# A hybrid decoder layer: reordering the opening's queues, and tying the users of side transfers to TensorE's place

## The chip, the cores and the metric

The kernel runs on one NeuronCore of a Trainium2 chip. The metric is the device time of one execution, in microseconds (us). The core has five engines with an instruction queue each, which work in order: PE (TensorE, the matmuls; its weight loads are listed as PEld), DVE (VectorE), ACT (ScalarE), POOL (GpSimd) and SP (SyncE). Transfers between HBM and the on-chip buffers (DMA) are issued from the queues of SP, ACT and POOL. An engine's waiting issue holds up everything behind it in that queue.

## The reference

One layer of a decoder over 2048 positions and 1024 channels, in 32-bit floats. Cut to what matters:

```python
mod = silu(c) @ w_ada + b_ada
shift, scale, gate = split(mod, 3)
h = rms_norm(x, norm_g) * (1 + scale) + shift
hq, hf, hi, hz, rq, rk, rv, rz, ga, gb = split(h @ w_in, offsets)     # ten column groups, 9216 columns
uA = head_rms_norm(hgrn2(silu(hq), lb + (1 - lb) * sigmoid(hf), hi)) * silu(hz)
uB = head_rms_norm(retention(rotary(rq), rotary(rk), rv)) * silu(rz)
m = sigmoid(ga) * uA + sigmoid(gb) * uB
out = rms_norm(x + gate * (m @ w_out), final_g)
```

`hgrn2` is a gated linear recurrence with 8 heads of 128 channels, `retention` a recurrence with a fixed decay for each of 8 heads. Both are computed in chunks.

## The kernel before

**Numbers and products.** Each 32-bit operand of a large product is split into two parts in a rounded format, hi and lo: ScalarE rounds (L340, `b<-w` or `A<-h`), VectorE subtracts (L341). A product is three matmuls, hi x hi, hi x lo and lo x hi.

**Quads.** The combined projection is cut into quads: for each half of the sequence (1024 positions, two blocks of 512) and for each head or pair of heads, a block of columns named by kind (a, v, b, A, B) and number. The string `ORDER` gives their order within a half. Quad 0 (`a0`) is computed as plain products in `opening()`. Every later quad takes seven products of combined operands in place of eight (`seq` lists them). The combinations of h are called A11, A12, A22, S1 to S4; those of the weights are summed in place by `Weights.add` (L466). Each product is four steps of three matmuls, and its result is evicted by `after` (L528 on ScalarE; L541, L548, L552 on VectorE) and handed to `deliver`.

**What sets the order.** TensorE's instructions keep the order in which the program traces them (class `InOrder`; `PE.last` is the latest). The queues of the other engines are ordered when the program is built: a planner simulates the execution and lets each engine take, of the instructions that are ready in that simulation, the one with the lowest place. Three means steer it:

- `tc.high_priority(offset=n)` moves what is traced inside n places ahead.
- `pin(ins)` (`tc.keep_in_program_order`) puts an instruction behind whatever was traced before it on its own engine.
- `behind(ins, pe)` puts an instruction behind a given one, here one of TensorE's. `tc.issue_after(ins)` does so for everything traced inside the block on the engine of `ins`. Both give an order of issue in the planner's simulation and no wait on the chip.

**The opening.** For each of the eight 128-row tiles of the first half, `stats` squares and sums a row tile on ScalarE (L1185); POOL makes 1/rms and a diagonal matrix of it (L186, L189, L1188). `turned` multiplies rows by that diagonal on TensorE (`xps`), which transposes and normalizes at once, and ScalarE applies scale and shift (L1210). These come from `ada`: VectorE multiplies a tile of `w_ada` (`wa`, 512 KB, loaded on SP by `ada_load`) by silu(c) broadcast to all partitions (`scb`, from `row_of_c`: eight products `dgs` at L387, a matmul `scp`, two copies at L393), with a running sum (L400, L404). `prepare(tb, s)` does this for block tb and the s-th channel tile of the order `KO`. Then `plain_step` multiplies with quad 0's weights `wp`, which `plain_split` loads on ScalarE's queue and splits. In the same loop quad 1's first two products run. At the end `deliver` evicts quad 0 (sigmoids at L625, scalings at L627 and L630, products at L635) and frees the banks.

**Buffers.** `tp` has six tiles of 512 columns that side work and evictions share, `mu` four, `r` six for raw weights (`NR`), `bw` three for split weights.

**Side work.** `Background.tick` is called at each product step; after every four it advances each generator in `side` by one `yield`. `next_h(1)` makes the second half's h in the first half: it loads x (`xt`), squares it on ScalarE (L1109), loads the transposed x (`xT`), multiplies (L1125) and scales it, stores it, loads it again and combines it (L1145 to L1161). `ada_row(0)` and `ada_row(1)`, in the second half, make the row `gate`: for each of eight tiles they load 256 KB (`wg`, L1322), yield twice, and add weight times silu(c) to an accumulator (L1328).

The rotary tables of each b quad (`ct`, `sn`) are loaded on POOL's queue into `tp` tiles.

Of the kernel before, what the change touches and what calls it, by code (L numbers as in the profile page):

```python
# [10 lines left out]
F32R = mybir.dt.float32r  # L11
# [52 lines left out]
def tile_hybrid(ctx: ExitStack, tc: tile.TileContext, a: dict, out: bass.AP):  # L64
# [268 lines left out]
    def halves(t):  # L333
        return t[:, 0, :], t[:, 1, :]

    def a_tile(name):
        return halves(apool.tile([P, 2, 512], F32R, name=name, tag="A", bufs=NA))

    def split_into(t, src):
        S.activation(out=t[0], in_=src, func=AF.Copy)  # L340
        return V.tensor_tensor(out=t[1], in0=src, in1=t[0], op=ALU.subtract)  # L341

# [28 lines left out]
    mods = cpool.tile([P, 2 * KT], F32, name="mods", tag="mods")  # L371

    def ada_load(kt):
        made = []
        for i in range(2):
            w = apool.tile([P, 1024], F32, name=f"wa{kt}_{i}", tag="A", bufs=NA)
            nc.sync.dma_start(out=w, in_=a["w_ada"][kt, i])
            made.append(w)
        return made

    def row_of_c():
        scb = apool.tile([P, 1024], F32, name="scb", tag="A", bufs=NA)
        dgs = apool.tile([P, 1024], F32, name="dgs", tag="A", bufs=NA)
        for i in range(2):
            dg = dgs[:, i * 512 : (i + 1) * 512]
            for k4 in range(4):
                V.tensor_scalar(  # L387
                    out=dg[:, k4 * P : (k4 + 1) * P], in0=ident, scalar1=sc[:, 4 * i + k4 : 4 * i + k4 + 1], scalar2=None,
                    op0=ALU.mult,
                )  # L390
            ps = bank(f"scp{i}", ("v", "lv")[i])
            PE.matmul(out=ps, lhsT=ones, rhs=dg, start=True, stop=True)
            V.tensor_copy(out=scb[:, i * 512 : (i + 1) * 512], in_=ps)  # L393
        return scb
# [33 lines left out]
    class Weights:  # L428
# [36 lines left out]
        def add(self, out, x, y):  # L465
            V.tensor_tensor(out=out, in0=x, in1=y, op=ALU.add)  # L466

# [628 lines left out]
    def next_h(sb):  # L1096
        for tb in range(NBLK):
            b = sb * NBLK + tb
            rb = tmp(f"rb{b}")
            for t in range(4):  # L1100
# [7 lines left out]
                for i in range(2):  # L1108
                    pin(S.activation(out=xt[i], in_=xt[i], func=AF.Square, accum_out=ss[:, i : i + 1]))  # L1109
                r = upool.tile([P, 2], F32, name=f"xr{b}_{t}", tag="rr", bufs=4)  # L1110
# [9 lines left out]
            for kt in range(KT):  # L1120
                x = tmp(f"xT{b}_{kt}")
                nc.sync.dma_start(out=x, in_=a["x_t"][kt, :, b * BLK : (b + 1) * BLK])
                for _ in range(3):
                    yield
                pin(V.tensor_tensor(out=x, in0=x, in1=rb, op=ALU.mult))  # L1125
                S.activation(out=x, in_=x, func=AF.Identity, scale=amul[kt], bias=modp[kt])
                htd[tb, kt] = dram(f"hT{b}_{kt}", [P, 512])
                nc.sync.dma_start(out=htd[tb, kt], in_=x)
        for j in range(4):
# [14 lines left out]
            yield  # L1144
            pin(V.tensor_tensor(out=h22, in0=h21, in1=h22, op=ALU.subtract))  # L1145
            keep("S1", h22)
# [3 lines left out]
            yield  # L1150
            pin(V.tensor_tensor(out=h21, in0=h11, in1=h21, op=ALU.subtract))
            keep("S3", h21)
# [6 lines left out]
            yield  # L1159
            pin(V.tensor_tensor(out=h12, in0=h12, in1=h11, op=ALU.add))  # L1160
            keep("S4", h12)  # L1161
# [12 lines left out]
    def opening():  # L1174
# [71 lines left out]

        was = {0: ada_load(0), 4: ada_load(4)}
        for t in range(4):
            stats(t)
        for t in range(4, 8):  # L1250
            load_rows(t)
        plain = {}
# [11 lines left out]

        for b in (0, 1):
            plain_split(b)
        prepare(0, 0)
        for b in (2, 3):
            plain_split(b)
        W.load()  # L1270
        W.split(part_tile("b1_1", "cc", NCC))
        W.split(halves(upool.tile([P, 2, 512], F32R, name="b2_1", tag="af", bufs=1)))
        two = pp.tile([P, 2, 512], F32, name="c01_y1", tag="rt", bufs=1)
        acc = {(0, 0): bank("c00", "o"), (1, 0): bank("c10", "o"), (1, 1): bank("c11", "x0"), (0, 1): two[:, 0, :]}
        xb[1], yb[1] = bank("x1", "x1"), two[:, 1, :]
        for s in range(KT + 2):
            if s < 2:
                for t in (4 + 2 * s, 5 + 2 * s):
                    stats(t)
            if s == 5:  # L1280
                tables()
# [4 lines left out]
            if 0 <= s - 1 < KT:  # L1286
                prepare(1, s - 1)
            if s < KT:
                kt = KO[s]
                for ch in range(2):  # L1290
                    plain_step(acc[ch, 0], 2 * (kt // 4) + ch, ats[0, kt], kt)
                m, j = 1 + kt // 4, kt % 4
                product_step(yb[1] if m == 2 else xb[1], m, 1, j, j == 0, j == 3)
# [10 lines left out]
        for ch, tb in ((0, 0), (1, 1), (1, 0), (0, 1)):  # L1304
            with tc.high_priority(offset=FIRSTS if ch else PEV):
                deliver(0, ch, tb, acc[ch, tb])
# [11 lines left out]
    def ada_row(j):  # L1318
        acc = upool.tile([P, 512], F32, name=f"acc{j}", tag="mu", bufs=4)
        for kt in range(KT):  # L1320
            w = tmp(f"wg{j}_{kt}")
            nc.sync.dma_start(out=w, in_=a["w_gate"][j, kt])  # L1322
            yield
            yield
            if kt == 0:
                V.tensor_scalar(out=acc, in0=w, scalar1=sc[:, 0:1], scalar2=None, op0=ALU.mult)
            else:
                V.scalar_tensor_tensor(out=acc, in0=w, scalar=sc[:, kt : kt + 1], in1=acc, op0=ALU.mult, op1=ALU.add)  # L1328
        bgt = tmp(f"bg{j}")
# [234 lines left out]
```

## Time and profile before

| | |
|---|---|
| runs | 2019.73, 2016.7, 2019.8 us; median 2019.73 |
| profiled execution | 2015.04 us; span from first to last instruction 2013.3 us |
| granted TensorE clock, mean | 0.993 |
| busy TensorE | 1930.3 us |
| busy VectorE, ScalarE, POOL | 1420.3, 985.7, 296.6 us |
| moved by DMA | 259.97 MB |

The profile is of one execution. An engine's idle time is put down to the instruction or transfer that ended it. A number after L is a line of the kernel. Times within the span count from its first instruction. A granted clock under 1.00 in a stretch means that TensorE's matmuls ran slower there.

### The profile page before, as it was taken

The numbers are of one execution on the slowest core, as the hardware profiler recorded it, in microseconds if no ns is written. First come the engines' busy times: TensorE is split into PE (matmuls) and PEld (weight loads), VectorE is DVE, ScalarE is ACT, GpSimd is POOL, SyncE is SP. The second block draws the span as 40 slices with busy tenths as digits, with TensorE's granted clock in tenths as the row PEclk, the third lists the DMA queues.
The fourth block names the chain that finished last, engine by engine and source line by source line (L and its number), as shares of the span: only waits on it lengthen the run. The fifth ranks groups of instructions, "written<-read, shape, count | busy, mean of one in ns | idle before, by whom it ended". The sixth has DMA issues, their size and how long they took to land.

```text
span 2013.3 us, 40043 instructions
## 1 busy us (share of the span) xinstructions
PE 1930.3 (96%) x15172; PEld 1581.7 (79%) x15172; DVE 1420.3 (71%) x2677; ACT 985.7 (49%) x2426; POOL 296.6 (15%) x522
## 2 busy tenths in 40 slices
PE   5799899999999999999999999989999999999998
PEld 4578788887788778888888788878788888887887
DVE  6796767666767777778977676777767775878332
ACT  5635444554556446556444545544454446454321
POOL 2002210211113211201002110211021102010000
PEclk9999999999999999999999999999999999999999
DMA  9335524354354564546544433454435433336442
GB/s 301 78 92 137 134 60 117 102 133 123 112 162 118 133 159 150 168 149 219 134 116 130 112 89 93 121 136 146 111 100 132 114 79 117 91 115 201 152 145 84
DMA packets 453122, 259.97 MB, mean 129 GB/s; under 512 B 171713, under 2 KB 406209, under 8 KB 452929
## 3 DMA queue, kind: packets, MB, share of 16 engines
q1 hardware_dynamic: 286752, 172.89, 30.3%
q10 hardware_dynamic: 153120, 76.04, 13.4%
q0 software_dynamic: 13056, 8.47, 1.7%
q8 instruction: 120, 1.97, 0.4%
q14 instruction: 74, 0.60, 0.1%
HBM read 188.03 MB, written 69.21 MB: 128 GB/s over the span
## 4 chain that ended last, share of the span: by engine, by line
PE 82%; DMA 8%; DVE 5%; ACT 2%; issue 1%; POOL 1%; SPq 1%; ACTq 0%; POOLq 0%; DVEq 0%
PE x L77 33%; PE v L77 17%; PE ops L77 9%; PE y L77 8%; PE E L77 4%; PE lv L77 3%; PE R L77 3%; PE uT L80 2%; DMA rd<-c 1%; DMA ud<-ur 1%; DVE b L341 1%; DVE w L466 1%; PE F L77 1%; DMA sn<-lin 1%; ACT b L340 1%
## 5 line engine op out<-in xcount | busy, mean ns | idle before, releaser
L341 DVE TENSOR_TENSOR b<-w,b 128x512 fp32r<-128x512 f32 (+1 forms) x553 | 346.8, 635 | 228.1 <-ACT b L340 219.5
L340 ACT ACTIVATE b<-w 128x512 fp32r<-128x512 f32 (+1 forms) x553 | 317.1, 583 | 298.3 <-PE x L77 243.0
L77 PE MATMUL x<-S,b 128*128 128x512 f32 x1704 | 432.5, 399 | 7.7 <-DVE c L548 7.7
L77 PE MATMUL v<-S,b 128*128 128x512 f32 x1704 | 424.3, 397 | 3.4 <-ACT c L528 2.4
L77 PE MATMUL x<-A,b 128*128 128x512 f32 x1704 | 421.6, 395 | 0.9 <-DVE c L552 0.9
L77 PEld LDWEIGHTS v<-S,b 128*128 128x128 f32 x1704 | 317.6, 190 | 72.0 <-ACT c L528 3.5
L77 PEld LDWEIGHTS x<-A,b 128*128 128x128 f32 x1704 | 315.7, 188 | 67.5 <-ACT m L345 1.3
L77 PEld LDWEIGHTS x<-S,b 128*128 128x128 f32 x1704 | 312.5, 189 | 70.6 <-DVE c L548 7.0
L77 PE MATMUL y<-A,b 128*128 128x512 f32 x840 | 208.3, 396 | 1.0 <-DVE ro L695 0.8
L466 DVE TENSOR_TENSOR w<-w,w 128x512 f32<-128x512 f32 x284 | 195.4, 688 | 9.6 <-DMA w<-in_w_b_dram 4.8
L186 POOL TENSOR_SCALAR ssh<-ssh 128x1 f32<-128x1 f32 x128 | 51.2, 400 | 999.5 <-ACT uh L883 999.4
L77 PEld LDWEIGHTS y<-A,b 128*128 128x128 f32 x840 | 155.9, 189 | 35.3 <-issue 1.8
L77 PE MATMUL ops<-wo,m 128*128 128x512 f32 x768 | 174.5, 390 | 0.0
L77 PEld LDWEIGHTS ops<-wo,m 128*128 128x128 f32 x768 | 144.1, 188 | 29.8
L528 ACT ACTIVATE c<-v 128x512 f32<-128x512 f32 x142 | 84.6, 596 | 149.6 <-PE v L77 134.4
L888 ACT ACTIVATE uh<-E,rrh 128x128 f32<-128x128 f32 x128 | 47.3, 369 | 111.6 <-POOL rrh L189 97.4
L77 PEld LDWEIGHTS lv<-q,k 128*32 128x32 f32 (+1 forms) x5888 | 70.2, 109 | 37.6 <-issue 28.5
L189 POOL TENSOR_TENSOR rrh<-ssh,mhalf 128x1 f32<-128x1 f32 x128 | 97.7, 763 | 10.6
L548 DVE TENSOR_TENSOR c<-c,x 128x512 f32<-128x512 f32 x71 | 48.8, 687 | 63.8 <-PE x L77 63.6
L77 PE MATMUL lv<-q,k 128*32 128x16 f32 (+2 forms) x5888 | 81.3, 188 | 11.8 <-DVE k L856 5.6
L855 DVE TENSOR_TENSOR q<-q,f 128x512 f32<-128x512 f32 x112 | 77.9, 695 | 8.9 <-PE lv L77 8.5
L528 ACT ACTIVATE c<-y 128x512 f32<-128x512 f32 x70 | 41.8, 597 | 73.7 <-PE y L77 73.6
(191 smaller groups left out, 2431.7 us busy)
## 6 DMA issues: line engine op xcount, KB each, us to landing
w<-in_w_d_dram ACTq DMA_DIRECT2D x128, 256.0 KB
w<-in_w_c_dram ACTq DMA_DIRECT2D x66, 256.0 KB
mu<-ud SPq DMA_DIRECT2D x64, 256.0 KB
w<-in_w_a_dram ACTq DMA_DIRECT2D x60, 256.0 KB
wa<-in_w_ada_dram SPq DMA_DIRECT2D x16, 512.0 KB
w<-in_w_b_dram ACTq DMA_DIRECT2D x32, 256.0 KB
vd<-vt SPq DMA_DIRECT2D x128, 64.0 KB
vh<-vd SPq DMA_DIRECT2D x64, 128.0 KB
```

What stands on the lines that cost most here:

```text
L77: return self.kept(nc.tensor.matmul(**kw))
L80: return self.kept(nc.tensor.transpose(**kw))
L186: G.tensor_scalar(out=ss, in0=ss, scalar1=n * EPS, scalar2=None, op0=ALU.add)
L189: G.tensor_tensor(out=dst, in0=ss, in1=mhalf.broadcast_to([P, w]), op=ALU.pow)
L340: S.activation(out=t[0], in_=src, func=AF.Copy)
L341: return V.tensor_tensor(out=t[1], in0=src, in1=t[0], op=ALU.subtract)
L466: V.tensor_tensor(out=out, in0=x, in1=y, op=ALU.add)
L528: S.activation(out=t, in_=ps, func=AF.Copy)
L548: V.tensor_tensor(out=t, in0=t, in1=xb[q], op=ALU.subtract)
L855: V.tensor_tensor(out=qv, in0=qv, in1=tv[:, :, :, 0:1].broadcast_to([P, NU, nb, m]), op=ALU.mult)
L888: behind(S.activation(out=dsts[i], in_=pos[i], func=AF.Copy, scale=rr[:, i : i + 1]), PE.last)
```

## The change

1. **The opening's queues.** The first channel tile's two `wa` loads are traced at high priority, so that they may go first on SP; the second pair and the last four row tiles of x are queued behind them on SP. All four plain weights are loaded and split before the first `prepare`, with their VectorE subtractions queued behind the last of the `dgs` products; quad 1's raw weights are loaded there too. Quad 1's first two splits are queued behind the first A tile's two parts, on VectorE and on ScalarE.
2. **The sums of quad 1's weights** (`Weights.add`, while fewer than eight splits are done) are placed behind TensorE's latest instruction at step 2 of the opening's loop.
3. **The end of the opening.** What `deliver` puts on ScalarE's queue for quad 0 is queued behind the rounding of the last tile of h that `prepare` made.
4. **Users of side transfers.** In `next_h` and `ada_row` the instruction that first uses a loaded tile is placed behind TensorE's latest instruction.
5. **The gates' weights.** `ada_row` yields four times between load and use, not twice.

No arithmetic changes.

```diff
     def split_into(t, src):
-        S.activation(out=t[0], in_=src, func=AF.Copy)
-        return V.tensor_tensor(out=t[1], in0=src, in1=t[0], op=ALU.subtract)
+        parted["hi"] = S.activation(out=t[0], in_=src, func=AF.Copy)
+        parted["lo"] = V.tensor_tensor(out=t[1], in0=src, in1=t[0], op=ALU.subtract)
+        return parted["lo"]
...
-            nc.sync.dma_start(out=w, in_=a["w_ada"][kt, i])
+            sent["wa"] = nc.sync.dma_start(out=w, in_=a["w_ada"][kt, i])
...
-                V.tensor_scalar(
+                sent["dgs"] = V.tensor_scalar(
                     out=dg[:, k4 * P : (k4 + 1) * P], in0=ident, scalar1=sc[:, 4 * i + k4 : 4 * i + k4 + 1], scalar2=None,
...
         def add(self, out, x, y):
-            V.tensor_tensor(out=out, in0=x, in1=y, op=ALU.add)
+            ins = V.tensor_tensor(out=out, in0=x, in1=y, op=ALU.add)
+            if self.nsplit < 8:
+                behind(ins, self.mark)
+
+        mark = None
...
-                    pin(S.activation(out=xt[i], in_=xt[i], func=AF.Square, accum_out=ss[:, i : i + 1]))
+                    behind(pin(S.activation(out=xt[i], in_=xt[i], func=AF.Square, accum_out=ss[:, i : i + 1])), PE.last)
...
-                pin(V.tensor_tensor(out=x, in0=x, in1=rb, op=ALU.mult))
+                behind(pin(V.tensor_tensor(out=x, in0=x, in1=rb, op=ALU.mult)), PE.last)
...
-            pin(V.tensor_tensor(out=h22, in0=h21, in1=h22, op=ALU.subtract))
+            behind(pin(V.tensor_tensor(out=h22, in0=h21, in1=h22, op=ALU.subtract)), PE.last)
...
-        was = {0: ada_load(0), 4: ada_load(4)}
+        with tc.high_priority(offset=FIRSTS):
+            was = {0: ada_load(0)}
         for t in range(4):
             stats(t)
-        for t in range(4, 8):
-            load_rows(t)
+        with tc.issue_after(sent["wa"].ins):
+            was[4] = ada_load(4)
+            for t in range(4, 8):
+                load_rows(t)
...
-        for b in (0, 1):
-            plain_split(b)
+        with tc.issue_after(sent["dgs"].ins):
+            for b in range(4):
+                plain_split(b)
+        W.load()
         prepare(0, 0)
-        for b in (2, 3):
-            plain_split(b)
-        W.load()
-        W.split(part_tile("b1_1", "cc", NCC))
-        W.split(halves(upool.tile([P, 2, 512], F32R, name="b2_1", tag="af", bufs=1)))
+        firsts = dict(parted)
+        with tc.issue_after(firsts["lo"].ins), tc.issue_after(firsts["hi"].ins):
+            W.split(part_tile("b1_1", "cc", NCC))
+            W.split(halves(upool.tile([P, 2, 512], F32R, name="b2_1", tag="af", bufs=1)))
...
+            if s == 2:
+                W.mark = PE.last
...
                 prepare(1, s - 1)
+                W.behind = dict(parted)
...
-            with tc.high_priority(offset=FIRSTS if ch else PEV):
+            with tc.high_priority(offset=FIRSTS if ch else PEV), tc.issue_after(W.behind["hi"].ins):
                 deliver(0, ch, tb, acc[ch, tb])
...
-            yield
-            yield
+            for _ in range(4):
+                yield
             if kt == 0:
                 V.tensor_scalar(out=acc, in0=w, scalar1=sc[:, 0:1], scalar2=None, op0=ALU.mult)
             else:
-                V.scalar_tensor_tensor(out=acc, in0=w, scalar=sc[:, kt : kt + 1], in1=acc, op0=ALU.mult, op1=ALU.add)
+                behind(
+                    V.scalar_tensor_tensor(out=acc, in0=w, scalar=sc[:, kt : kt + 1], in1=acc, op0=ALU.mult, op1=ALU.add),
+                    PE.last,
+                )
```

Two more pinned users in `next_h` (the lines that were L1151 and L1160) are changed in the same way.

More of the change, by code (lines that the diff above doesn't have):

```diff
@@ L337, in a_tile @@
         return halves(apool.tile([P, 2, 512], F32R, name=name, tag="A", bufs=NA))
+    parted = {}
     def split_into(t, src):
-        S.activation(out=t[0], in_=src, func=AF.Copy)
-        return V.tensor_tensor(out=t[1], in0=src, in1=t[0], op=ALU.subtract)
+        parted["hi"] = S.activation(out=t[0], in_=src, func=AF.Copy)
+        parted["lo"] = V.tensor_tensor(out=t[1], in0=src, in1=t[0], op=ALU.subtract)
+        return parted["lo"]
     def split_here(t):
@@ L371, in tile_hybrid @@
     mods = cpool.tile([P, 2 * KT], F32, name="mods", tag="mods")
+    sent = {}
     def ada_load(kt):
@@ L1150, in next_h @@
             yield
-            pin(V.tensor_tensor(out=h21, in0=h11, in1=h21, op=ALU.subtract))
+            behind(pin(V.tensor_tensor(out=h21, in0=h11, in1=h21, op=ALU.subtract)), PE.last)
             keep("S3", h21)
@@ L1159, in next_h @@
             yield
-            pin(V.tensor_tensor(out=h12, in0=h12, in1=h11, op=ALU.add))
+            behind(pin(V.tensor_tensor(out=h12, in0=h12, in1=h11, op=ALU.add)), PE.last)
             keep("S4", h12)
```

## The prediction, made before the result was known

> **What bounds the kernel now.** I read the page first, then TensorE's waits stretch by stretch, then the order of time around each long one.
>
> ```profile
> PE 1930.3 (96%) x15172; PEld 1581.7 (79%) x15172; DVE 1420.3 (71%) x2677; ACT 985.7 (49%) x2426; POOL 296.6 (15%) x522
> ```
>
> TensorE is busy for 1930 of 2013 us, so at most some 83 us of idle time can go. TensorE's waits from 0 to 110 us (total, times, longest):
>
> ```profile
> PE scp L77 <- DVE dgs L387: 11.4, 1, 11.4
> PE xps L77 <- ACT h L1210: 9.7, 2, 8.7
> PE x L77 <- DVE c L548: 5.2, 1, 5.2
> PE c L77 <- ACT A L340: 5.0, 1, 5.0
> ```
>
> That is 31 us of the 83, so the opening is where most of the idle time sits. Sums by stretch (start:end, length, then busy time of PE, PEld, DVE, ACT, POOL, granted clock, DMA share, GB/s):
>
> ```profile
> 2.00:8.00 6.00, 0.00 (x0) 0.00 (x0) 1.35 (x10) 2.99 (x4) 0.00 (x0) 1.00 0.97 273
> 8.00:14.00 6.00, 2.57 (x3) 1.18 (x4) 4.07 (x12) 5.83 (x11) 4.22 (x8) 1.00 1.03 395
> 14.00:20.00 6.00, 3.26 (x10) 1.78 (x8) 4.33 (x8) 1.26 (x2) 2.35 (x5) 1.00 1.05 330
> 26.00:32.00 6.00, 5.20 (x17) 4.25 (x18) 2.06 (x4) 4.64 (x9) 5.24 (x9) 1.00 1.13 235
> 50.00:75.00 25.00, 22.57 (x125) 18.50 (x124) 24.33 (x44) 15.29 (x26) 0.96 (x1) 1.00 0.37 85
> 80.00:85.00 5.00, 4.58 (x9) 2.88 (x10) 4.86 (x9) 2.77 (x7) 0.00 (x0) 0.50 0.00 0
> 1356.00:1361.00 5.00, 5.00 (x20) 4.24 (x20) 2.61 (x6) 2.71 (x8) 1.32 (x2) 0.72 0.56 167
> ```
>
> Until about 20 us the transfers run near 330 to 395 GB/s: the opening waits for bytes, and their order matters. From 50 to 75 us VectorE is full. A long stop of TensorE is also paid a second time, in a lower clock: 0.50 after the 5.0 us wait, 0.72 after the later one at 1351 us.
>
> **Part 1, the start of the opening.** Rows in order of time (start, duration, idle time before and its releaser):
>
> ```profile
> 6.59 0.17 DVE L168 TENSOR_TENSOR sc<-sc,cT 128x8 f32<-128x8 f32 x1
> 10.39 1.77 DVE L387 TENSOR_SCALAR dgs<-ident,sc 128x128 f32<-128x128 f32 x8
> 15.25 0.69 DVE L393 COPY scb<-scp 128x512 f32<-128x512 f32 x1 [0.94 <-PE scp L77]
> 16.04 2.04 PE L77 MATMUL xps<-diag,xrow 128*128 128x128 f32 x8 [0.83 <-POOL x0r L189]
> 22.11 0.63 ACT L340 ACTIVATE b<-w 128x512 fp32r<-128x512 f32 x1 [3.57 <-DMA w<-in_w_c_dram]
> 23.38 0.15 DVE L404 SCALAR_TENSOR_TENSOR mods<-mods,ng 128x1 f32<-128x1 f32 x1
> 25.98 0.76 ACT L1210 ACTIVATE h<-xps,mods 128x512 f32<-128x512 f32 x1
> ```
>
> The first transposed rows are done at 16.04 + 2.04 = 18.1 us, but the modulation that scales them (L404) comes at 23.4, and ScalarE's scaling (L1210) at 26.0: both queues first serve quad 1's weight pieces, which land at 22.1. The change sends the first two `wa` tiles ahead of everything on SP, puts all eight `dgs` products ahead of the plain weights' subtractions on VectorE, and queues quad 1's two splits behind the first A tile's. Then the modulation no longer sets the start. Its new price: `cT` now lands behind two `wa` tiles (1.05 MB, about 3 us at 330 to 395 GB/s), so the product of its sigmoid (L168) moves from 6.6 to about 9.5 us; from the first diagonal at 10.39 to the end of the second copy at 15.94 are 5.6, so 15.1; two `wa` reductions (1.28 each, L400's row below) and L404 add 2.7: about 18 us. What sets the start instead is the fourth row of x. Sizes from the issues:
>
> ```profile
> wa<-in_w_ada_dram SPq DMA_DIRECT2D x16, 512.0 KB
> xrow<-in_x_dram SPq DMA_DIRECT2D x8, 512.0 KB
> wp<-in_w_a_dram ACTq DMA_DIRECT2D x4, 256.0 KB
> ```
>
> Before, four rows and three `wp` are 2.9 MB; with 273 GB/s for 6 us (1.64 MB) and then 395, they are through at 11.1 us. After, the two `wa` come on top, 3.9 MB: 13.8 us. If the fourth `wp` and the two pieces of quad 1 also go ahead (ScalarE's queue now holds six loads in a row), 4.7 MB: 16.2 us. So the rows are 2.7 to 5.1 us later and the transposes end at 20.8 to 23.2 instead of 18.1; the scaling can follow at once instead of at 26.0. Gain 2.8 to 5.2 us; I take 4. It is nothing, or a loss of about 2, if ScalarE's in-order loads block its squares; 6.5 at best, were the rows hardly late. The Trainium skill, "DMA: Bandwidth & Descriptors", section "Issuing engines are not separate DMA queues", says that transfers started by different engines run on the same 16 DMA engines and interleave. By that rule no gain comes from bandwidth, only from order, and the 16.2 us end (gain 2.8) is the nearer one. The stretch rows, at one rate whoever issues, agree.
>
> ```profile
> 34.45 1.28 DVE L400 CUSTOM_DVE_ANT_0 wa<-wa,scb,bad 128x1024 f32<-128x1024 f32 x1 [2.00 <-DMA wa<-in_w_ada_dram]
> 26.99 0.69 DVE L466 TENSOR_TENSOR w<-w,w 128x512 f32<-128x512 f32 x1 [1.05 <-DMA w<-in_w_c_dram]
> ```
>
> The next modulation waits 2.0 us for `wa`, after a stretch (26 to 32 us) with 235 GB/s. With rows and `wa` ahead of the other weights I take 1 us more (0 to 2). The weight sums at L466, held behind TensorE's place at step 2, free 1 us of waiting near 27 us but fall as two 0.69 us operations into VectorE's full stretch: nothing either way, 1.4 us if uncovered.
>
> **Part 2, the end of the opening.**
>
> ```profile
> 73.85 0.78 ACT L1210 ACTIVATE h<-xps,mods 128x512 f32<-128x512 f32 x1 [0.96 <-PE xps L77]
> 74.65 1.28 ACT L625 ACT_TABLE_LOAD   x1
> 80.16 2.14 PE L77 MATMUL c<-A,bp 128*128 128x512 f32 x3 [4.95 <-ACT A L340]
> 82.97 1.29 DVE L635 TENSOR_TENSOR q<-c,sg 128x512 f32<-128x512 f32 x2
> 83.72 3.92 PE L77 MATMUL y<-A,b 128*128 128x512 f32 x12
> ```
>
> The last tile of h is there at 74.6, yet its rounding (A L340), which ends TensorE's wait at 80.2, stands behind quad 0's sigmoids and their table load. The change queues those behind it, so TensorE goes on at about 75.5 instead of 80.2. Late next: the sigmoid and product that free the bank of `c11` for `y`. from 75.3 ScalarE needs the table (1.28) and four operations of a tile (a sigmoid, two scalings, the sigmoid of `c11`; 0.78 each by L1210's row, at most): 79.7; then the product, 1.29 / 2. `y` comes at about 80.3, not 83.7. Gain 3.4, say 3.5 (1 if quad 2's weight splits come first, 5 at best). The clock at 0.50 over 4.58 us of work cost 2.3; the stop that stays is shorter than 4, so I take 1.5 (0 to 2.6). The Trainium skill, "TensorE: Matmul & The Clock Gate", section "What's actually happening", puts TensorE at half clock after an idle window of about 3.4 us. The row (0.50 after 4.95) agrees; by the rule alone the saving would be the whole 2.3, and the opening's sum 0.8 better. The 5.2 us wait at 102 us hangs on a weight of quad 2 loaded through ScalarE's queue, which the change does not touch: kept.
>
> Opening together: 4 + 1 + 3.5 + 1.5 = 10 us.
>
> **Part 3, the gates' weights.** Instructions of the tile, the chain, and waits from 1318 to 1370 (the PE rows from 1300 to 1430):
>
> ```profile
> L1322 SPq DMA_DIRECT2D wg<-in_w_gate_dram x16: 333/428/1454, 1278.2 to 1400.4; - x16
> 1333.68 10.31 DMA wg<-in_w_gate_dram
> DVE acc L1328 <- DMA wg<-in_w_gate_dram: 5.5, 1, 5.5
> PE R L77 <- DVE st L966: 4.7, 1, 4.7
> PE v L77 <- DVE b L341: 0.9, 1, 0.9
> POOL sn L682 <- DVE acc L1328: 4.4, 1, 4.4
> ```
>
> One late weight stops VectorE for 5.5 us, and behind it weight splits, rotations and the state update; TensorE loses 4.7 + 0.9 = 5.6, and 0.28 x 5.0 = 1.4 by clock. From the first to the last load are 16 + 5 + 14 = 35 side steps in 122.2 us, 3.5 us each. Two more steps put the use 7.0 us later, past the 5.5 that were missing. Price: 28 + 4 more steps, some 112 us longer, with one of the six `tp` buffers and one of four `mu` buffers held; the row end moves to about 1525, far ahead of the output stage. `mu` was shared with the accumulator in the same way under two quads already, and there no transpose of u shows among TensorE's waits. I take 5.5 of the 7.0 (0 to 7).
>
> **Part 4, the side stage that makes the second half's h.** Waits from 400 to 980, the PE rows from 420 to 800:
>
> ```profile
> DVE xT L1125 <- DMA xT<-in_x_t_dram: 3.2, 2, 2.7
> ACT xt L1109 <- DMA xt<-in_x_dram: 2.5, 1, 2.5
> DVE sw L693 <- DMA sn<-lin: 5.8, 2, 3.1
> PE R L77 <- DVE st L966: 4.2, 2, 2.4
> PE uT L80 <- ACT c L528: 3.4, 2, 2.9
> ```
>
> Tying the users behind TensorE's last traced instruction adds no wait, only a later place in VectorE's and ScalarE's queues; behind them stand evictions and state updates. It can remove the 5.7 us of the first two rows, of which I see TensorE paying about 2. The table waits (`sn`) stay. I take 2 (loss of 3 to gain of 4).
>
> **Sum.** 10 + 5.5 + 2 = 17.5. Every reordered queue moves other small stops; one stop of 2 to 3 us and its like I set against it: 3.5. Net 14 us. The profiled execution took 2015.0 us; 2001. The runs shown are 1.7 to 4.8 above it; I add 3: **2004 us**.
>
> **Rivals.** *VectorE eats the opening.* It has 24.33 of 25 us busy from 50 to 75; if `wa` still arrives at 34 us, the earlier start only lengthens the wait in the middle, and the last combinations come no sooner. The opening then gives 2, the sum is 2 + 5.5 + 2 - 3.5 = 6: 2009 + 3 = 2012. Against it: the 2 us wait for `wa` in that very queue. *It does not do what it says.* If queue order in the program, not place, leaves the users late, or new stops fill the freed time, at most 2 us move: 2017. *Slower: the tables.* A side tile held longer makes the rotary tables late, since they take `tp` buffers on POOL's queue (4.4 us in the row above, behind the gates' weight). There are two tables in each of four b quads beside the side stages; one late table cost TensorE 2.4 (longest `R` wait), with the waits behind it some 3. Six more late ones are 18 us; with the opening's 10 and no gain from parts 3 and 4, less 3.5, that is +11.5 on 2015: 2026 + 3 = 2029; from three more late tables on the change is slower. Against it: only two were late under the longer side stage.
>
> **Chances.** Forecast 0.52, with its own range 1993 to 2010 (best ends: 6.5 + 2 + 5 + 2.6 + 7 + 4 less 3.5, and what the low ends leave); VectorE 0.20; no effect 0.12; tables or another stop like them 0.16. Differences under 0.2% (4 us) cannot be told from none. Faster: 0.51 + 0.18; within: 0.01 + 0.02 + 0.11; the rest slower, with 0.01 of no effect. Range 1993 to 2021: it leaves out the worst tables and little else.
>
> **What would show it.** Part 1: L1210's first row near 22 us, with `wa` issued before `cT`; wrong if a square or scaling waits on ScalarE for a weight load. Part 2: no TensorE wait on `A L340` near 70, `y` some 8 us earlier than 83.7; wrong if VectorE ends the idle time there. Part 3: no wait of `acc` on `wg`, loads spread over about 230 us. Part 4: no `xt`, `xT` waits; `sn` waits not above 6 us. The forecast fails if stops of the `sn` kind grow, or if the first `y` is not earlier.

## The result: slower, outside the forecast's range

| | before | after |
|---|---|---|
| median of five runs each | 2019.73 us | 2029.41 us |
| ratio, 95% interval | | 1.0057 [1.0040, 1.0074] |
| profiled execution | 2015.04 us | 2029.07 us |
| span | 2013.3 us | 2027.3 us |
| mean granted clock | 0.993 | 0.987 |

The change costs some 11.5 us; 2004 us was forecast. The slower rival had put 2029 on the clock, but not, as will be seen, for the reason it gave. (The changed lines shift the numbers: L340, L341, L966 of before are L342, L343, L975 after.)

The page's totals after:

```profile
PE 1939.5 (96%) x15172; PEld 1587.7 (78%) x15172; DVE 1421.7 (70%) x2677; ACT 986.5 (49%) x2426; POOL 295.4 (15%) x522
```

No engine has more work. TensorE's busy time rises by 9 us with the same matmuls: these ran at a lower clock. TensorE's waits from 0 to 110 us after (total, times, longest):

```profile
PE xps L77 <- ACT h L1219: 11.6, 2, 11.3
PE scp L77 <- DVE dgs L392: 8.2, 1, 8.2
PE xps L77 <- POOL x0r L189: 3.9, 1, 3.9
PE xps L77 <- POOL diag L1197: 2.3, 2, 2.0
PE c L77 <- ACT A L342: 1.4, 2, 1.2
PE y L77 <- DVE q L644: 1.4, 1, 1.4
```

The products `dgs` came 3.2 us earlier (8.2 for 11.4), and the wait at the opening's end shrank from 5.0 to 1.2, as meant. The waits for POOL's 1/rms (`x0r`) and for its diagonal grew, from 0.8 to 3.9 and from 0.5 to 2.3. The wait for the first scaled rows is 11.3 for 8.7, but that is not shown to be the change: in traces of kernels whose start is that of before it lies between 8.7 and 11.3 too. The wait of 5.2 us at 102 us (`x` on `c`), which the prediction kept, has shrunk to 0.7. Waits from 400 to 980 us, where the second half's h is made:

```profile
PE lv L77 <- DVE k L868: 7.5, 4, 2.7
PE y L77 <- DVE xr L1120: 6.8, 1, 6.8
PE v L77 <- ACT c L537: 2.2, 1, 2.2
DVE sw L702 <- DMA sn<-lin: 9.1, 2, 5.0
```

The two answering rows of before, from the same view:

```profile
PE lv L77 <- DVE k L859: 1.7, 2, 1.0
PE y L77 <- DVE ro L695: 0.8, 1, 0.8
```

The waits of the squares and products for their loads (`xt` 2.5, `xT` 3.2 us before) are gone from the list, and worse ones have come. Four of the stretches shown for before, and the one of the new stop, with the granted clock as the third figure from the end:

```profile
8.00:14.00 6.00, 3.78 (x4) 1.17 (x4) 2.53 (x8) 5.06 (x10) 3.37 (x8) 1.00 0.92 255
50.00:75.00 25.00, 22.66 (x123) 19.07 (x123) 23.41 (x44) 14.65 (x25) 0.00 (x0) 0.93 0.36 84
80.00:85.00 5.00, 3.54 (x19) 2.51 (x18) 3.79 (x7) 3.92 (x7) 0.00 (x0) 1.00 0.00 0
1356.00:1361.00 5.00, 5.00 (x28) 4.30 (x27) 4.92 (x9) 2.75 (x7) 0.81 (x2) 1.00 0.66 168
480.00:490.00 10.00, 3.21 (x13) 2.34 (x12) 4.31 (x9) 5.12 (x12) 1.00 (x2) 0.72 0.40 125
```

The slow clock after 75 us (0.50 before) and at 1356 us (0.72) is gone with the stops ahead of it, and around a new stop of 6.8 us at 482 us it is 0.72. From 90 to 97 and from 97 to 103 us it is 0.88 and 0.85, although no stop there is longer than 1.4 us.

TensorE runs its matmuls in nearly the same order in all of these kernels, so the start of one matmul can be set against its start in the trace of before. In us, positive is later:

| matmul, start before | after | opening alone | next_h alone | gates alone | after without next_h |
|---|---|---|---|---|---|
| `xps`, 39.05 | +6.1 | +5.4 | +1.7 | +0.8 | +7.6 |
| `c_y`, 70.88 | +7.2 | +7.1 | +3.5 | +2.7 | +9.0 |
| `x`, 105.41 | +0.2 | -0.3 | +1.6 | +1.9 | +1.9 |
| `x`, 480.02 | +0.3 | -3.1 | +4.5 | -0.8 | -1.2 |
| `y`, 484.56 | +7.9 | -3.5 | +11.0 | -1.3 | -1.6 |
| `R`, 701.91 | +2.2 | -0.2 | +4.9 | +2.6 | +1.3 |
| `v`, 868.79 | +15.1 | -0.1 | +17.8 | +2.7 | +1.4 |
| `y`, 1340.01 | +15.8 | -1.2 | +18.8 | +2.1 | +1.2 |
| `R`, 1376.52 | +8.0 | -1.6 | +18.3 | -5.7 | -6.6 |
| `lv`, 1430.71 | +13.5 | -1.6 | +19.8 | -1.5 | -2.6 |

One column is one execution. Where the code up to a place is that of before, columns still differ by 1 to 4 us, and the profiled execution of before lies 5 us under its median; so amounts are taken from ratios, and places from traces. The opening comes out even; 15 us are lost from 480 to 870 us; 8 are won at the gates' stop and 5.5 of them lost again by 1431 us. (About 1 us of that gain and of that loss is no stop: the two matmuls `gps` at the end of the gates' row stand at 1375.7 us before and at 1440.8 after.) The stop at 482 us is the longest, but not what lasts: by 702 us only 2 us of it are left, as the trace of after lacks waits that before has on the way (`uT` 3.4 us before, 0.7 after). The other 13 come between 702 and 870 us. A second trace of the changed kernel goes the same way: +7.9 at `y`, +1.5 at `R`, +14.1 at `v`.

### The profile page after: what moved, and what is told of

Same layout as the page of the kernel before. It is cut to its first block, busy times and chain, and to the rows that moved or that the text cites. A ratio compares the mean times of both kernels' runs of the same rounds, so it can differ in the third digit from the quotient of the medians.

```text
span 2027.3 us, 40037 instructions
## 1 busy us (share of the span) xinstructions
PE 1939.5 (96%) x15172; PEld 1587.7 (78%) x15172; DVE 1421.7 (70%) x2677; ACT 986.5 (49%) x2426; POOL 295.4 (15%) x522
## 4 chain that ended last, share of the span: by engine, by line
PE 82%; DVE 6%; DMA 6%; ACT 2%; issue 1%; POOL 1%; SPq 0%; ACTq 0%; POOLq 0%; DVEq 0%
PE x L77 33%; PE v L77 17%; PE y L77 9%; PE ops L77 9%; PE E L77 4%; PE lv L77 3%; PE R L77 3%; PE uT L80 1%; DMA rd<-ro 1%; DVE b L343 1%; DMA rd<-c 1%; DVE w L471 1%; PE F L77 1%; ACT b L342 1%; DMA ud<-ur 1%
## 5 line engine op out<-in xcount | busy, mean ns | idle before, releaser
L343 DVE TENSOR_TENSOR b<-w,b 128x512 fp32r<-128x512 f32 (+1 forms) x553 | 346.6, 635 | 238.4 <-ACT b L342 229.9
L342 ACT ACTIVATE b<-w 128x512 fp32r<-128x512 f32 (+1 forms) x553 | 316.7, 583 | 294.5 <-PE x L77 246.6
L864 DVE TENSOR_TENSOR q<-q,f 128x512 f32<-128x512 f32 x112 | 77.6, 693 | 11.4 <-PE lv L77 10.9
```

Of the source, the lines that this page charges most:

```text
L342: parted["hi"] = S.activation(out=t[0], in_=src, func=AF.Copy)
L343: parted["lo"] = V.tensor_tensor(out=t[1], in0=src, in1=t[0], op=ALU.subtract)
L864: V.tensor_tensor(out=qv, in0=qv, in1=tv[:, :, :, 0:1].broadcast_to([P, NU, nb, m]), op=ALU.mult)
```

## The experiments

Ratios are to the kernel before, run on the same chip; 0.1% is 2 us.

| run | what it is | ratio, 95% interval |
|---|---|---|
| e1_open | before + opening (parts 1 to 3 of the change) | 0.9976 [0.9962, 0.9989] |
| e2_side | before + the five later places in `next_h` | 1.0050 [1.0033, 1.0068] |
| e3_gates | before + `ada_row`'s edits | 0.9985 [0.9969, 1.0001] |
| e4_wafirst | after, `wa` really first | 1.0031 [1.0017, 1.0045] |
| f1_noside, f1_again | after without `next_h`'s places | 0.9954 [0.9936, 0.9971], 0.9979 [0.9965, 0.9993] |
| after_again | after | 1.0057 [1.0037, 1.0077] |
| s_xt, s_xT, s_comb | one kind of place each | 1.0025 [1.0011, 1.0040], 1.0019 [1.0004, 1.0034], 1.0012 [0.9997, 1.0026] |
| d_early | after, the five places one step earlier | 0.9980 [0.9967, 0.9993] |
| e_end | before + the end of the opening | 0.9967 [0.9950, 0.9984] |
| g_end_gates, g_again | before + end of the opening + gates | 0.9953 [0.9936, 0.9971], 0.9953 [0.9940, 0.9967] |
| e3b_steps | before + four steps, no tie | 1.0024 [1.0005, 1.0043] |
| o_loads, o_rows | opening, two mends of its start | 0.9983 [0.9968, 0.9998], 0.9992 [0.9979, 1.0005] |
| h_best | o_rows + gates | 0.9983 [0.9971, 0.9995] |

### Which part costs: e1_open, e2_side, e3_gates

Each applies only its own lines of the change to the kernel before.

```diff
# e1_open: split_into, ada_load, Weights.add, opening() as changed
# e2_side: only these places, five in all
-                    pin(S.activation(out=xt[i], in_=xt[i], func=AF.Square, accum_out=ss[:, i : i + 1]))
+                    behind(pin(S.activation(out=xt[i], in_=xt[i], func=AF.Square, accum_out=ss[:, i : i + 1])), PE.last)
# e3_gates: only ada_row
-            yield
-            yield
+            for _ in range(4):
+                yield
```

> The kernel before with only the opening's edits (queues, sums, end). Theory A (the loss of about 13 us arises in the side stage that makes the second half's h, the opening nets nothing): within 2 us of the kernel before; the scaling of the first h tile near 28 us, 6 us lost by 41 us, all of it back by 165 us, and no TensorE stop of 6.8 us near 485 us. Rival B (the opening's edits shift the planned order of all that follows, and the stops in the side stage come from that): 8 to 15 us slower than before, with the long stops near 485, 730 and 875 us.

> The kernel before with only the users of side transfers in next_h placed behind TensorE's latest instruction. Theory A: 12 to 17 us slower than before, the opening as before, the stops near 485, 700 to 770 and 870 us as in the changed kernel. Rival B: within 2 us of before.

> The kernel before with only ada_row's edits (four steps, users behind TensorE). Theory A: 1 to 4 us faster than before: the 5.6 us stop at 1348 to 1356 and its low clock go (about 7), and some 4 to 5 us come back as stops 75 to 95 us later. Rival B: 6 to 7 us faster, since the later stops come from the shifted order before it.

Measured: the opening gives 5 us, the gates 3, and the five places cost 10. The stop at `y` is in the run with the places alone (TensorE 11.0 us late at 484 us, 4.5 at 480) and not in that with the opening alone (-3.5 and -3.1): the theory that the places did it stands, and the one that the later opening did it falls. Two amounts were missed: the opening was to net nothing, and the places were to cost 12 to 17.

### Taking the places out again: f1_noside, after_again, f1_again

```diff
# f1_noside and f1_again: all five places so; after_again: no edit
-                behind(pin(V.tensor_tensor(out=x, in0=x, in1=rb, op=ALU.mult)), PE.last)
+                pin(V.tensor_tensor(out=x, in0=x, in1=rb, op=ALU.mult))
```

> The changed kernel without the five later places in next_h (opening and gates kept). Theory A (the five places alone cost the time: the run with them alone was 10 us slower than before, the one with the opening alone 4 us faster, the one with the gates alone 2 us faster): the effects add, 6 us faster than before (range 3 to 9), ratio about 0.997, and no stop of TensorE over 4 us between 480 and 490 us. Rival B (the opening's later h shifts all of the side work so that stops come back without those places too): not faster than before.

> The changed kernel as it is, on the chip of the next run, which is the same without the five later places in next_h. On other chips the parts gave 0.9954 (opening and gates) and 1.0050 (the five places), whose product is 1.0004, while the whole gave 1.0057. Theory (the parts add, since the five places reorder VectorE, ScalarE, POOL and SP in the same rows with and without the other parts; the traces put their cost at 13 to 16 us in both): ratio to before 1.000 to 1.004, and 14 us (0.7%) above the run without the places. Rival (they interact): 1.0057 again, and 20 us above it.

> The changed kernel without the five later places in next_h, beside the changed kernel on the same chip. Theory (the parts add): 0.9954 again, 14 us below the changed kernel. Rival (they interact): 20 us below it.

On one chip the changed kernel has a median of 2028.76 us and the same without the places 2014.09: 15 us, as the traces say (15 between `x` at 105 and `y` at 1340 us). The places alone had cost 10 (7 to 14), and the three parts alone multiply to 1.0011 where the whole measured 1.0057 twice. So the 14 us between the two kernels was met, the ratio of 1.000 to 1.004 was missed, and the kernel without the places has 0.9979 on this chip, not 0.9954 again; by these numbers 5 us (beside the run without the places) to 9 us (beside the product of the parts) of the whole are not the sum of its parts. The 5 lie within the uncertainty of the two ratios, and one kernel's ratio moved by 0.0025 between two chips; whether the parts interact, and in which queue, stays open.

### Which of the places: s_xt, s_xT, s_comb

```diff
# s_xt: the squares (ScalarE) alone; s_xT: the products (VectorE) alone; s_comb: the three combinations alone
+                    behind(pin(S.activation(out=xt[i], in_=xt[i], func=AF.Square, accum_out=ss[:, i : i + 1])), PE.last)
+                behind(pin(V.tensor_tensor(out=x, in0=x, in1=rb, op=ALU.mult)), PE.last)
+            behind(pin(V.tensor_tensor(out=h22, in0=h21, in1=h22, op=ALU.subtract)), PE.last)
```

> The kernel before with the later place for the squares of x alone (ScalarE). Theory A1 (each kind of user costs in its own stretch, as the run with all five showed them: some 3 us that last from 430 to 700 us, with a stop near 485 us on the way): 2 to 4 us slower than before, with ScalarE's evictions behind the squares late near 485 us. Rival A2 (the cost hangs on the interplay of all five places in the planner's order of VectorE): within 1.5 us of before.

> The kernel before with the later place for the multiplication of the transposed x alone (VectorE). Theory A1 (own stretch, 702 to 776 us): 5 to 8 us slower than before, lost between 700 and 780 us in stops of TensorE at the evictions of VectorE that stand behind the multiplications. Rival A2 (interplay): within 1.5 us of before.

> The kernel before with the later place for the first users of the loaded combinations alone (three instructions of VectorE, four times). By what is left of the run with all five places (10 us) when the squares (5 us) and the multiplications (4 us) are taken off: 1 us slower, at most 4. By the traces, which show 4 us lost between 800 and 925 us in the run with all five, in a wait of `lv` for a tree product of VectorE: 4 us slower (ratio 1.002).

Each costs by itself, 5, 4 and 2 us (the last within its uncertainty), and together 11 us, about what all five do (10): no interplay among them is needed, though one of some 6 us would not show. And each has its stop in its own stretch. TensorE's waits in the run with the squares, 430 to 900 us:

```profile
PE y L77 <- DVE xr L1111: 7.4, 1, 7.4
```

In the run with the products, 700 to 800 us:

```profile
PE lv L77 <- DVE k L859: 3.4, 2, 2.1
```

In the run with the combinations, 800 to 960 us (no such row before):

```profile
PE lv L77 <- DVE k L859: 2.7, 1, 2.7
```

### How a later place costs: d_early

The five users stay tied to TensorE's place, but to that of one step of the side work earlier.

```diff
-                for _ in range(3):
-                    yield
+                for _ in range(2):
+                    yield
+                mark = PE.last
+                yield
...
-                behind(pin(V.tensor_tensor(out=x, in0=x, in1=rb, op=ALU.mult)), PE.last)
+                behind(pin(V.tensor_tensor(out=x, in0=x, in1=rb, op=ALU.mult)), mark)
```

> The changed kernel with the five users of next_h tied to TensorE's place one step of the side work earlier (some 3.5 us), not to its latest instruction. Theory A (what costs is how late the users are placed: the chain of a table, a reduction or an eviction behind them gets late): half of the cost or more goes, 6 to 12 us faster than the changed kernel. Rival B (any tie to TensorE's place costs, since it keeps the users from being fitted in where the engine is free): within 3 us of the changed kernel.

All of it is gone: 2014.85 us beside 2028.76, as without the ties (2014.09). It is the lateness by one step, some 3.5 us, that costs, not the tie as such. But the early tie also wins nothing over no tie, though it shortens the waits for the loads (`xt` from 1.8 to none, `xT` from 1.6 to 1.4 us, beside the kernel without ties). How the lateness costs is seen in the order of time around 482 us. First before (VectorE's queue):

```profile
481.07 0.69 DVE L694 TENSOR_TENSOR sw<-x,sn 64x512 f32<-64x512 f32 x1
481.80 0.69 DVE L695 TENSOR_TENSOR ro<-x,ct 128x512 f32<-128x512 f32 x1
...
486.00 0.69 DVE L341 TENSOR_TENSOR b<-w,b 128x512 fp32r<-128x512 f32 x1 [2.66 <-ACT b L340]
```

Then after, with the end of ScalarE's wait and TensorE's next matmul:

```profile
486.20 0.60 ACT L537 ACTIVATE c<-v 128x512 f32<-128x512 f32 x1 [4.27 <-DMA rd<-c]
487.35 0.69 DVE L343 TENSOR_TENSOR b<-w,b 128x512 fp32r<-128x512 f32 x1 [3.99 <-ACT b L342]
488.07 0.69 DVE L704 TENSOR_TENSOR ro<-x,ct 128x512 f32<-128x512 f32 x1
488.91 2.47 PE L77 MATMUL y<-A,b 128*128 128x512 f32 x5 [6.79 <-DVE xr L1120]
```

And with the place one step earlier:

```profile
481.41 0.69 DVE L704 TENSOR_TENSOR ro<-x,ct 128x512 f32<-128x512 f32 x1
482.24 3.00 PE L77 MATMUL y<-A,b 128*128 128x512 f32 x12 [0.45 <-DVE ro L704]
486.54 0.69 DVE L343 TENSOR_TENSOR b<-w,b 128x512 fp32r<-128x512 f32 x1 [3.59 <-ACT b L342]
```

All three kernels have the same wait: ScalarE's eviction of `v` needs a tile that the store of rotated keys (`rd<-c`) still reads, and the weight split behind it on ScalarE, and so its other half on VectorE, come at 486 to 487 us. Before, and with the earlier place, the rotation `ro`, which frees the bank that `y` needs, stands ahead of that split on VectorE and never meets the wait. With the later place the planner put the split ahead of `ro`: an old wait off the path became TensorE's. The squares themselves are not what anyone waits for, though the list of waits puts the 6.8 us down to `xr`, their sum, which ended last.

The other kind of stop, which makes most of the lasting loss, has a cause as small. Before, in VectorE's queue:

```profile
758.11 0.69 DVE L748 TENSOR_TENSOR c<-c,c 128x512 f32<-128x512 f32 x1
758.71 0.27 DVE L859 TENSOR_TENSOR k<-k,f 128x64 f32<-128x64 f32 x1
```

After, with the matmul that waited:

```profile
765.19 0.68 DVE L757 TENSOR_TENSOR c<-c,c 128x512 f32<-128x512 f32 x1
...
769.27 0.69 DVE L471 TENSOR_TENSOR w<-w,w 128x512 f32<-128x512 f32 x1
769.87 0.26 DVE L868 TENSOR_TENSOR k<-k,f 128x64 f32<-128x64 f32 x1
770.28 0.69 PE L77 MATMUL lv<-q,k 128*16 128x16 f32 x64 [2.15 <-DVE k L868]
```

A tree product of 0.27 us, which `lv` waits for, came right behind `c<-c,c`; now six operations of 0.7 us stand between them. TensorE's waits of `lv` for such products are 7.5 us after, 1.7 before and 1.0 with the place one step earlier. Why the planner puts these six ahead is not shown.

### The opening's start: e4_wafirst, o_loads, o_rows, h_best

```diff
# e4_wafirst (after): the first pair of wa traced ahead of row_of_c
         with tc.high_priority(offset=FIRSTS):
+            was = {0: ada_load(0)}
             scb = row_of_c()
# o_loads (opening alone): as before, two plain weights and quad 1's raw weights behind the first prepare
-            for b in range(4):
+            for b in (0, 1):
                 plain_split(b)
-        W.load()
         prepare(0, 0)
+        for b in (2, 3):
+            plain_split(b)
+        W.load()
# o_rows (opening alone; h_best adds ada_row's edits)
+        for t in range(4, 8):
+            load_rows(t)
         with tc.issue_after(sent["wa"].ins):
             was[4] = ada_load(4)
-            for t in range(4, 8):
-                load_rows(t)
```

> The changed kernel with the first two wa loads traced ahead of row_of_c, whose two tiles come from the same pool tag; in the changed kernel they were issued at 12.7 us, after ten small and large loads, though traced at high priority. Theory A (the slot order of the pool held them back, and the late modulation sets the start): wa is issued first on SP, the first scaling of h stands at 20 to 23 us in place of 28.4, the time is 4 to 8 us below the changed kernel (2 to 6 above the kernel before). Rival C (ScalarE's weight loads, which wait for earlier transfers, set the start): the scaling stays at 26 to 28 us and the time within 2 us of the changed kernel.

> The kernel before with the opening's edits, but with the third and fourth plain weight and quad 1's raw weights loaded after the first preparation, as before, so that only two weight loads stand in a row on ScalarE's queue. Theory (these loads hold ScalarE's squares and scalings up): the trace is 3 us or more nearer to the kernel before at 41 us than the run with the opening alone (which was 6 behind), and the time 2 to 4 us below that run's ratio (0.9976), at 0.996. Rival (the later rows of x set the start): still some 6 us behind at 41 us, and a ratio of 0.9976 as before.

> The kernel before with the opening's edits, but with the last four row tiles of x no longer queued behind the first two wa pairs on SP (only the second pair is). Theory (the first scaling of h stands behind the square of the fifth row on ScalarE, and that row is issued at 20.8 us behind four wa tiles, 5.9 us before): the first scaling comes at 24 to 26 us instead of 28.4, the second block's first transposes lose their wait for the diagonal, the trace is 3 to 6 us ahead of the run with the opening alone at 41 us and at 74 us, ratio 0.995 to 0.996. Rival (the transfers' sum sets the start: what the rows win the wa tiles lose): within 2 us of the run with the opening alone at 74 us, ratio 0.9976.

> The same opening with the gates' edits, next_h as before: the candidate to beat the version that has the old start, the new end and the gates' edits (0.9953). Theory: 2 to 4 us below it, ratio 0.994. Rival: 0.995 to 0.9965, as the run with the whole opening and the gates.

The rows after, in order of time:

```profile
12.74 6.89 SPq L382 DMA_DIRECT2D wa<-in_w_ada_dram  x4
20.83 7.00 SPq L153 DMA_DIRECT2D xrow<-in_x_dram  x4
22.17 0.16 DVE L409 SCALAR_TENSOR_TENSOR mods<-mods,ng 128x1 f32<-128x1 f32 x1
27.35 1.06 ACT L1194 ACTIVATE sqj<-xrow 128x1024 bf16<-128x1024 f32 x1 [11.83 <-DMA w<-in_w_c_dram]
28.40 0.76 ACT L1219 ACTIVATE h<-xps,mods 128x512 f32<-128x512 f32 x1
63.97 0.91 SPq L382 DMA_DIRECT2D wa<-in_w_ada_dram  x2
68.11 1.28 DVE L405 CUSTOM_DVE_ANT_0 wa<-wa,scb,bad 128x1024 f32<-128x1024 f32 x1 [0.66 <-DMA wa<-in_w_ada_dram]
```

And two of before:

```profile
2.94 3.51 SPq L153 DMA_DIRECT2D xrow<-in_x_dram  x5
57.98 0.91 SPq L377 DMA_DIRECT2D wa<-in_w_ada_dram  x2
```

`wa` was not first: it is issued at 12.7 us (9.4 before), behind all of SP's small loads and `dT`. The modulation is ready at 22.2 us, but the first scaling stands on ScalarE behind the square of the fifth row, and that row, which was issued in the first five before, is now issued at 20.8. With `wa` truly first (e4, issued at 0.7 us) the first scaling comes at 26.4 us, not at 20 to 23, again behind the square of the fifth row, which is issued at 20.5; the second block's first transposes come 2 us earlier than after. Its ratio is 1.0031 for 1.0057, the two intervals overlapping: neither theory had both the scaling and the time. Moving ScalarE's loads back (o_loads) did not test what it was meant to: the planner issued them at the same times, 11.8 us without work ahead of the square again, and the start was as late. What these loads cost stays untested.

The 28.4 us by itself shows little: ten traces of kernels with the old start have this scaling between 26.0 and 28.7 us, seven with the new start between 27.1 and 28.5. o_rows put the fifth row back among the first five, and the first scaling came at 25.0 us (25.6 in h_best), ahead of all of them. Its trace:

```profile
2.96 3.56 SPq L153 DMA_DIRECT2D xrow<-in_x_dram  x5
24.96 0.76 ACT L1219 ACTIVATE h<-xps,mods 128x512 f32<-128x512 f32 x1
61.21 2.58 SPq L678 DMA_DIRECT2D lin<-tab  x4
63.84 1.09 SPq L382 DMA_DIRECT2D wa<-in_w_ada_dram  x2
67.97 1.28 DVE L405 CUSTOM_DVE_ANT_0 wa<-wa,scb,bad 128x1024 f32<-128x1024 f32 x1 [2.09 <-DMA wa<-in_w_ada_dram]
73.33 2.08 PE L77 MATMUL xps<-diag,xrow 128*128 128x128 f32 x8 [4.48 <-ACT h L1219]
```

It was 3 to 7 us ahead of the opening alone from 38 to 75 us, and 0.6 ahead at 77: TensorE waits 4.5 us for a scaling that hangs on the last pair of `wa`, and that pair is issued at 63.8 us, right behind the table's rearrangements `lin` on SP; in the changed kernel it is issued at 64.0, before at 58.0. In this trace the start is not what sets the opening's end; the last `wa` pair is. That its place in SP's queue, not a buffer, holds it is the reading of the rows; no run moved it. The mended start gave nothing in time (0.9992, and 0.9983 with the gates): both theories of both runs had forecast a shorter time.

### The opening's end and the gates: e_end, g_end_gates, g_again, e3b_steps

```diff
# e_end (before): the last rounding of h is kept, and quad 0's delivery queued behind it
+                W.behind = dict(parted)
-            with tc.high_priority(offset=FIRSTS if ch else PEV):
+            with tc.high_priority(offset=FIRSTS if ch else PEV), tc.issue_after(W.behind["hi"].ins):
# g_end_gates, g_again: e_end and ada_row's edits.   e3b_steps (before): only the four yields
```

> The kernel before with the end of the opening alone (what quad 0's delivery puts on ScalarE's queue goes behind the last rounding of h). Theory: the end alone gives the 6 us by which the trace of the run with end and gates was ahead at 251 us, ratio 0.997. Rival (it is given back at the weight of quad 2 near 102 us): within 2 us of before.

> The kernel before with the end of the opening (quad 0's sigmoids behind the last rounding of h) and the gates' edits, and the start of the opening as it was. If the opening's start is what ate the gain of its end (the start was 5 to 7 us behind at 41 us, the end won 5 to 6 back), the end alone gives 4 to 5 us and the gates 2: 6 to 7 us faster than before, ratio 0.9965. Rival (what the end wins is given back at the next wait, for quad 2's weight at 102 us, whatever the start does): 2 to 3 us faster, the gates' share alone.

> The end of the opening and the gates' edits, with the start as before and next_h as before: on this chip beside its parts. Theory (parts add): 0.9953 again, 8 to 10 us faster than before. Rival (it was a chip's luck): 0.998, what the run with opening and gates gave on its second chip.

> The kernel before with four steps instead of two between load and use of the gates' weights, without the tie to TensorE's place. Theory (the two steps take the stop away): no wait of the accumulation on a weight between 1318 and 1370 us, and 2 to 3 us faster than before (ratio 0.9985), as with the tie. Rival (the planner places the use early all the same): the stop stays, ratio 1.000.

The end by itself gives 6.7 us, more than the whole opening (4.8); with the gates it is 9.5 us, the same on two chips: 2009.91 beside 2019.88 us. That is the best version, and both kernels are slower. The four steps without the tie were to be 2 to 3 us faster and are 4.8 us slower. VectorE's waits from 1310 to 1460 us in that run:

```profile
DVE acc L1328 <- DMA wg<-in_w_gate_dram: 12.5, 3, 6.5
```

So two more steps alone do not cure the late weight: in the same stretch before has 8.8 us in four waits, the longest 5.5. With steps and tie no such row is left. The tie with the old two steps was not run.

## Why the prediction was wrong, step by step

**Part 4, the side stage, is the step that failed.** "Adds no wait, only a later place in VectorE's and ScalarE's queues; behind them stand evictions and state updates" was costed at a gain of 2, with a loss of 3 at worst. It cost 10 us alone and 15 in the whole. The sentence named the danger and gave it no price. The waits that it was to remove did go, and nothing was won by it: the kernel with the places one step earlier, in which they are shorter too, takes as long as the one without ties. The sum counted the waits saved and not what the planner would place ahead of what: a rotation behind a split that waits on ScalarE (TensorE stops for 6.8 us), a tree product behind six operations (7.5 us of such waits for 1.7). The parts measured alone add up to a loss of 2 us (-4.8 - 3 + 10); the whole lost 11.5, and the difference stays open.

**The slower rival had the number for a wrong reason.** Six late tables at 3 us were to make 2029. The same two tables are waited for as before, 2.4 and 0.9 us longer (the first is issued on POOL 1.9 us later, 469.4 for 467.5). Most of the other stops that grew are of VectorE's order (`y`, `lv`), one of ScalarE's (`v`, 2.2 us). Its sign of failure, waits for `sn` above 6 us, did show (9.1), but does not tell the kernels apart: without the places (f1_again) and with the earlier ones (d_early) the same row has 6.3 and 6.5 us, and nothing is lost.

**Part 1, the start: no gain.** Forecast +4 and +1. The whole opening gives 4.8 and its end alone 6.7, so the start costs something between nothing and 5: with the gates, the whole opening and its end alone have 0.9954 and 0.9953 on one chip, but 0.9979 and 0.9953 when run again, each on another. In the traces the new start is 4 to 9 us behind at 70 us; traces with the old start are themselves up to 4 behind that of before. Three premises fell: `wa` is not ahead of everything on SP; the fourth row does not set the start, the fifth does, through ScalarE's order; and a gain at the start did not reach the end, where, as read above, the last `wa` pair decides. This last is near the rival in which `wa` comes no sooner, with SP's queue in VectorE's place. Nor did the bytes flow at one rate: 255 GB/s from 8 to 14 us, 395 before, with the DMA engines nearly as busy (0.92 and 1.03) and SP's small loads and `dT` ahead of `wa`; in o_rows, where three of the small loads still stand ahead of `wa` but a fifth row goes first and `dT` later, the same stretch moved 397 GB/s. So these three small loads alone do not make the low rate; which of the rest does is not shown. The Trainium skill, "DMA: Bandwidth & Descriptors", section "Issuing engines are not separate DMA queues", says that transfers from all engines interleave on the same 16 DMA engines. Nothing here speaks against it. But I had read one rate from it, "whoever issues", and no row bears that out: those of before already run from 235 to 395 GB/s, and none of them tells who issued.

**Part 2, the end: right in its mechanism, the sum partly by luck.** 3.5 + 1.5 forecast, 6.7 [3.2, 10.1] measured alone. The wait went from 5.0 to 1.2 us, and the stretch from 80 to 85 us has the clock at 1.00. The product that frees the bank came as the next wait, as said (`y` on `q`, 1.4 us). But in the trace of e_end the gain from `c_y` at 70.9 to `y` at 83.7 is 3.7 us, so the clock's 1.5 was not won on top by then; 3.4 more come by `x` at 105.4, where the 5.2 us wait that the prediction kept is 0.6. Why that one went is not shown. And `y` was to come 8 us earlier than 83.7; it came at 87.2, since the start was late. The clock agrees in two places with the Trainium skill, "TensorE: Matmul & The Clock Gate", section "What's actually happening" (half clock after an idle window of about 3.4 us): around the stop of 1.2 us it is 1.00, and around the new one of 6.8 us 0.72. From 90 to 103 us it does not: 0.85 to 0.88 without a stop above 1.4 us.

**Part 3, the gates: right in place, half in size, the cause incomplete.** TensorE's stop went: 7.8 us between `y` at 1340 and `R` at 1376. In time it is 3 us [0, 6], for 5.5; in the traces 4 to 5.5 are lost again by 1431 us, where `lv` now waits 2.4 us behind an accumulation. And I had given the gain to the two steps; without the tie they make the kernel slower.

## What to carry to other kernels

In a kernel whose queues are ordered by a planner, moving an instruction later is no free cover for its wait: price it by what the planner will put ahead of what in the same queue, above all small operations that TensorE waits for, and look for waits already in the trace that stand just off the path. If a user has to be tied to a place, tie it early: one step of 3.5 us decided between 15 us lost and none, and even the early tie was worth no more than no tie here. Before mending a stage's start, find the last thing its end needs and when that is issued.

## What was not expected of the hardware

Executions of one kernel differ in the opening by more than their ends do: the second block's transposes at 39 us came 7.6 us later than before in one trace of the kernel without the places and 2.2 in another, with ratios of 0.9954 and 0.9979 on two chips. A single trace of a stage bound by transfers is good for its order, not for its microseconds.

At the start of a trace the granted clock is not to be taken at its word: before, the stretch from 26 to 32 us has 1.00, yet the eight `xps` at 26.80 took 2.08 us, and sixteen at 43.99 took 1.95.
